# Trunk kernel in fp32r parts: one tile for a weight's high and low parts, eighteen block products in the wide form, parameters turned behind the last unit

## The chip, the cores and the metric

The kernel runs on 1 core of one Trainium2 chip. The metric is the device time of one execution in microseconds. The core's engines are TensorE (PE, matmuls; PEld, its weight loads), VectorE (DVE), ScalarE (ACT), GpSimd (POOL) and SyncE (SP); transfers run on DMA engines and are issued here by SyncE (loads) and GpSimd (accumulating transfers from on-chip memory to on-chip memory).

## The reference

The input x has 512 tokens of 1024 values, in float32. There are two layers. Each adds a mixer and then a gated feed-forward network (FFN, 2816 hidden values) to the residual stream; each of these starts with an RMS norm, and a final norm ends the trunk.

```python
proj = gelu(einsum('bsd,de->bse', xn, w_in_odd[i]))          # mixer of layer 1
u, v = proj[..., :C_WIDTH], proj[..., C_WIDTH:]              # 1024 each
mix = chunked_spatial_gating(u, v, sgu_norm[i], w_spatial[i], b_spatial[i])
h = h + einsum('bse,ed->bsd', mix, w_out_odd[i])

def gated_conv_ffn(x, w_gate, w_up, conv_w, conv_b, w_down):
    g = einsum('bsd,df->bsf', x, w_gate)
    g = causal_dwconv3(g, conv_w) + conv_b
    up = einsum('bsd,df->bsf', x, w_up)
    return einsum('bsf,fd->bsd', silu(g) * up, w_down)
```

## The kernel before

**Arithmetic.** Every float32 matrix product is made from fp32r matmuls. An operand is split into a high part (the value rounded to fp32r) and a low part (the rest), and three matmuls, high by high, high by low and low by high, are summed in PSUM (mm3, L153 to L157). Weights are loaded by SyncE as float32 (`raw_...`, four buffers). `parts` (L147) makes the high part on ScalarE and the low part on VectorE. `summed` (L136) makes the low part without VectorE: ScalarE writes the negated high part into it (L140), GpSimd issues a DMA that accumulates the float32 value onto it (L142), and ScalarE writes the high part (L144). High and low parts are tiles of their own, of tags `whi` and `wlo`, six buffers each.

**Block products.** The large products of the FFN's gate and up (key g and u) and of the mixer of layer 1 are made by a scheme of seven block products in place of eight (numbered 1 to 7; products 3, 5, 6 and 7 need sums of weight blocks, s12 and s34, and sums of activation blocks, t). One block product takes four steps of the contraction and has 256 token columns. `multiply` (L554) has two forms. The narrow one is mm3 four times, 12 matmuls of 256 columns (L577). The wide one takes high and low part of the moving operand as one operand of 512 columns: four matmuls with the high part of the stationary operand (L567) and four of 256 columns with its low part (L570). Its sum stands in both halves of a PSUM bank, and who reads it has to add the two. Products 1, 6, 7 and 4 go to a bank "a", 5 and 3 to "e", 2 to "b" (BANK, L552). Seven banks are shared by all matmuls, and one is kept for transposes and the like.

**FFN.** The loop goes over units f = 0, 2, ..., 20, two 128-row tiles of the hidden dimension each. f=0 is computed directly, f=2 by narrow products, f=4 with wide gate and narrow up products, and f=6 and later by wide ones alone (FIRST_WIDE, L550; in_both, L794). Within a unit the products run in the order g1 u1 g5 g2 g6 u5 u6 u2 g7 u7 g3 u3 g4 u4 (`products`, L781). Results are collected by a copy on ScalarE and additions on VectorE (L800, L812) into `rows` (gate) and `kept` (up); then follow a causal convolution (c: ScalarE L611, VectorE L613), silu (L621), the factor 1/rms (rstd_f; s times r is L827), and the product with up, whose parts are the operands `a_hi` and `a_lo` of the down product (`d` in layer 0, `dn` in layer 1). `prepare` (L730 to L771) makes the weights of a unit: a11 (product 1), s12g, s34g, s12u, s34u and the second halves; s12g and s34g of f=4 and later get their low parts by the accumulating DMA (L758 to L760). A matmul is written g_8e if it belongs to gate, f=8, bank e.

**Mixer of layer 1.** v and u are 1024 columns each. The second half of v (v1) and the first half of u (u0) are made by seven block products for each of two token halves i (InProducts, L969 to L1030), all narrow; here the activations are stationary and the weights move. `v_0e` is v1, i=0, bank e.

**Parameters.** Each layer's norm and convolution parameters are loaded as rows, turned by one TensorE transpose (L110) and copied by VectorE (L112). Layer 1's are asked for at L888, behind the units of layer 0's FFN and ahead of d_last, the down product of its last four tiles.

**Order.** A scheduler puts the instructions of an engine in order, by their dependencies and its own estimates, except where `behind` (L83) or `inorder` ties one instruction behind another. So an edit at one place can move instructions at others. The last part of the kernel (L1340 on) is written out by hand: `taken` adds a down product to y (L1183), `squared`, `halved` (L1300), `rooted` and `inverted` make the final norm of a token block.

## Time and profile before

| | |
|---|---|
| median of 3 runs | 975.89 us (975.62 to 975.98) |
| the profiled execution | 975.82 us, of which the span of instructions is 974.1 us |
| TensorE clock granted | 0.999 |
| transposes of parameters (L110) | 2, at 32.7 and 227.6 us |
| low parts by accumulating DMA, s12g | 18 transfers, 4.5 to 7.8 us to landing |
| mean DMA rate | 152 GB/s |

In the rows quoted below a line of a timeline has start, duration, engine, line, operation, output and inputs, and, in brackets, how long the engine was idle before it and what ended the idle time. A line of the chain has start, the time it adds to the chain, engine, tile and line; "issue" is time in which the engine waited for nothing that the profile shows. Layer 0's FFN lies from about 150 to 470 us, layer 1's mixer around 475 to 630 and its FFN from there to the end.

### The profile page before, as it was taken

Reading aid. Unit: us, or ns where it says so; the run is one execution under the profiler, and the core shown is the slowest. Engines: PE = TensorE matmul, PEld = TensorE weight load, DVE = VectorE, ACT = ScalarE, POOL = GpSimd, SP = SyncE. Lnnn points to the kernel's source line nnn. Section 1 sums busy time; section 2 is a strip of 40 time slices with the busy share of each in tenths; the row PEclk is TensorE's granted clock in tenths of the full one; section 3 lists DMA queues with packets and bytes.
Section 4 is the critical chain, followed back from the end, with each engine's and each line's share of the span. In section 5 each row is a group of like instructions: output and inputs, shape, how many; then the busy total and the mean of one; then the engine's idle time right before and its main releaser. Section 6 shows DMA issues by size and latency. Waiting matters only on the chain.

```text
span 974.1 us, 14029 instructions
## 1 busy us (share of the span) xinstructions
PE 964.4 (99%) x5144; PEld 829.1 (85%) x5144; DVE 816.9 (84%) x1387; ACT 596.8 (61%) x905; POOL 149.6 (15%) x173
## 2 busy tenths in 40 slices
PE   9999999999999999999999999999999999999996
PEld 7888888998888888888889988889988888888885
DVE  5887458989899998998887765589898989889897
ACT  5523347765676555765488734587665666656775
POOL 2141023110111011110310001221111011110123
PEclk9999999999999999999999999999999999999999
DMA  7442225776777677764324623167767777668775
GB/s 251 143 141 86 87 87 111 178 176 164 194 167 167 167 170 195 170 164 152 120 62 116 202 77 100 55 131 188 185 145 195 195 173 165 170 159 200 194 156 137
DMA packets 94417, 148.36 MB, mean 152 GB/s; under 512 B 5156, under 2 KB 60428, under 8 KB 94348
## 3 DMA queue, kind: packets, MB, share of 16 engines
q1 hardware_dynamic: 78316, 98.69, 32.1%
q0 software_dynamic: 14256, 46.93, 26.8%
q10 hardware_dynamic: 1776, 1.84, 0.5%
q8 instruction: 40, 0.66, 0.3%
q14 instruction: 29, 0.24, 0.1%
HBM read 98.42 MB, written 2.10 MB: 103 GB/s over the span
## 4 chain that ended last, share of the span: by engine, by line
PE 98%; DVE 1%; issue 0%; ACT 0%; POOLq 0%; DVEq 0%; POOL 0%
PE d L156 3%; PE dn L156 3%; PE dn L157 3%; PE d L157 3%; PE dn L155 3%; PE d L155 3%; PE gu L155 2%; PE gu L157 2%; PE oo L157 1%; PE gu L156 1%; PE oo L156 1%; PE oo L155 1%; PE oe L157 1%; PE oe L156 1%; PE oe L155 1%; PE u_2a L577 1%
## 5 line engine op out<-in xcount | busy, mean ns | idle before, releaser
L613 DVE SCALAR_TENSOR_TENSOR c<-rows,prm,c 128x512 f32<-128x512 f32 x88 | 65.8, 749 | 2.6 <-ACT c L611 1.5
L142 POOL DMA_DIRECT2D wlo_g<-raw_g x20 | 17.2, 859 | 313.2 <-DVE kept L800 146.4
L156 PE MATMUL dn<-wlo_dn,a_hi 128*128 128x512 f32 x144 | 56.2, 390 | 0.0
L156 PE MATMUL d<-a_lo,whi_d 128*128 128x512 f32 x144 | 56.2, 390 | 0.0
L157 PE MATMUL dn<-whi_dn,a_lo 128*128 128x512 f32 x144 | 56.2, 390 | 0.0
L157 PE MATMUL d<-a_hi,wlo_d 128*128 128x512 f32 x144 | 56.2, 390 | 0.0
L155 PE MATMUL dn<-whi_dn,a_hi 128*128 128x512 f32 x144 | 56.1, 390 | 0.0
L155 PE MATMUL d<-a_hi,whi_d 128*128 128x512 f32 x144 | 56.1, 390 | 0.0
L727 ACT ACTIVATE whi_a<-raw_g 128x512 fp32r<-128x512 f32 x20 | 12.6, 632 | 58.4 <-PE g_8e L567 8.5
L211 POOL TENSOR_TENSOR ssq_f<-ssq_f,sq_f 128x512 f32<-128x512 f32 x14 | 19.4, 1386 | 135.4 <-ACT sq_f L210 100.4
L140 ACT ACTIVATE wlo_g<-raw_g 128x1024 fp32r<-128x1024 f32 x20 | 21.2, 1061 | 29.1 <-PE g_2e L577 8.7
L200 ACT ACTIVATE hg<-h,prm 128x512 fp32r<-128x512 f32 x24 | 17.3, 722 | 34.8 <-DVE h L313 34.8
L621 ACT ACTIVATE s<-c,prm 128x512 f32<-128x512 f32 x44 | 31.5, 718 | 9.6 <-DVE c L613 9.5
L1183 DVE SCALAR_TENSOR_TENSOR y<-dn,small,y 128x512 f32<-128x512 f32 x40 | 28.0, 750 | 7.4 <-PE dn L157 7.4
L611 ACT ACTIVATE c<-rows,prm 128x512 f32<-128x512 f32 x44 | 31.4, 715 | 4.1 <-DVE rows L824 4.1
L201 DVE SCALAR_TENSOR_TENSOR hg<-h,prm,hg 128x512 fp32r<-128x512 f32 x24 | 23.6, 986 | 11.1 <-ACT hg L200 11.1
L157 PEld LDWEIGHTS d<-a_hi,wlo_d 128*128 128x128 f32 x144 | 27.0, 188 | 5.7
L157 PEld LDWEIGHTS dn<-whi_dn,a_lo 128*128 128x128 f32 x144 | 27.0, 188 | 5.7
L155 PEld LDWEIGHTS d<-a_hi,whi_d 128*128 128x128 f32 x144 | 27.1, 188 | 5.4
L155 PEld LDWEIGHTS dn<-whi_dn,a_hi 128*128 128x128 f32 x144 | 27.1, 188 | 5.4
L156 PEld LDWEIGHTS dn<-wlo_dn,a_hi 128*128 128x128 f32 x144 | 27.0, 188 | 5.4
L156 PEld LDWEIGHTS d<-a_lo,whi_d 128*128 128x128 f32 x144 | 27.0, 188 | 5.4
(1132 smaller groups left out, 3317.6 us busy)
## 6 DMA issues: line engine op xcount, KB each, us to landing
raw_g<-in_w_ffn_gate_dram SPq DMA_DIRECT2D x40, 512.0 KB, 4.0
raw_u<-in_w_ffn_up_dram SPq DMA_DIRECT2D x40, 512.0 KB, 3.8
raw_dn<-in_w_ffn_down_dram SPq DMA_DIRECT2D x22, 512.0 KB, 5.9
wlo_u<-raw_u POOLq DMA_DIRECT2D x21, 512.0 KB, 6.7
wlo_g<-raw_g POOLq DMA_DIRECT2D x20, 512.0 KB, 4.6
raw_d<-in_w_ffn_down_dram SPq DMA_DIRECT2D x18, 512.0 KB, 6.0
wlo_s12g<-s12g POOLq DMA_DIRECT2D x18, 512.0 KB, 6.1
wlo_s34g<-s34g POOLq DMA_DIRECT2D x18, 512.0 KB, 6.0
```

What stands on the lines that cost most here:

```text
L140: first = nc.scalar.activation(lo, raw, AF.Copy, scale=-1.0)
L142: nc.gpsimd.dma_start(lo, raw, accum_op=ALU.add)
L155: nc.tensor.matmul(ps, lhs[0], rhs[0], start=start, stop=False)
L156: nc.tensor.matmul(ps, lhs[0], rhs[1], start=False, stop=False)
L157: nc.tensor.matmul(ps, lhs[1], rhs[0], start=False, stop=stop)
L200: nc.scalar.activation(hg[k][0], h[k], AF.Copy, scale=g)
L201: nc.vector.scalar_tensor_tensor(hg[k][1], h[k], g, hg[k][0].bitcast(F32), op0=ALU.mult, op1=ALU.subtract)
L211: nc.gpsimd.tensor_tensor(self.ssq, self.ssq, sq, ALU.add)
L611: nc.scalar.activation(c, t[:, 0:S], AF.Copy, scale=prm("cf", ft))
L613: self.last_conv = nc.vector.scalar_tensor_tensor(c, t[:, i : S + i], prm("cf", i * NF + ft), c, op0=ALU.mult, op1=ALU.add)
L621: self.last_silu = nc.scalar.activation(s, c, AF.Silu, bias=self.prm("bf", ft))
L1183: return nc.vector.scalar_tensor_tensor(dst, ps, ffn.cols[:, t : t + 1], dst, op0=ALU.mult, op1=ALU.add)
```

## The change

High and low parts of a weight become one tile of tag `w` with six buffers, of the same size as the two before. A buffer is claimed and given back for both parts together. For the mixer's v1 and u0 the products 2, 5 and 3 take the wide form, with the weights' two parts as the moving operand, and the places that collect them add both halves. In the FFN the up products 2, 5 and 3 of f=4 become wide as well, in both layers; their second additions are those that `after` makes already for wide products. Layer 1's parameters are turned behind the last matmul of the last unit (f=20) of layer 0, by a tie on TensorE. At the end `taken(5, 1, right)` moves ahead of `halved` and `rooted` of block 2. TensorE has 5069 matmuls and transposes in the program where it had 5141, VectorE 1407 instructions where it had 1389; ScalarE's, GpSimd's and SyncE's counts are as before.

```diff
--- before.py
+++ after.py
@@ -74,11 +74,11 @@
             ("ffn", rows_of(norm_ffn[0]), NK), ("cf", conv_rows(conv_ffn[0]), 3 * NF),
             ("bf", rows_of(b_conv_ffn[0]), NF)])
 
-    def params1():
+    def params1(order):
         return params("1", [
             ("mix", rows_of(norm_mix[1]), NK), ("bsp", b_spatial[0], NK),
             ("ffn", rows_of(norm_ffn[1]), NK), ("cf", conv_rows(conv_ffn[1]), 3 * NF),
-            ("bf", rows_of(b_conv_ffn[1]), NF)])
+            ("bf", rows_of(b_conv_ffn[1]), NF)], order)
 
     def behind(ins, first):
 
@@ -93,8 +93,8 @@
     for t in range(PAD):
         nc.gpsimd.memset(inv_pos[:, t : t + 1], 1.0 / (t + 1))
 
-    def params(layer, rows_):
-        return params_fetch(layer, rows_, nc.sync)()
+    def params(layer, rows_, order=lambda ins: ins):
+        return params_fetch(layer, rows_, nc.sync)(order)
 
     def params_fetch(layer, rows_, queue):
         rows = sum(n for _, _, n in rows_)
@@ -109,7 +109,9 @@
             ps = aux_bank(f"prm_ps{layer}")
             order(nc.tensor.transpose(ps[:, :rows], pk[:rows, :], ident[:rows, :rows]))
             sb = cp.tile([P, P], F32, tag="prm0" if layer == "0" else "prm1", name=f"prm{layer}")
-            order(nc.vector.tensor_copy(sb[:, :rows], ps[:, :rows]))
+            ins = nc.vector.tensor_copy(sb[:, :rows], ps[:, :rows])
+            if order is inorder:
+                order(ins)
 
             def col(key, i):
                 return sb[:, views[key] + i : views[key] + i + 1]
@@ -133,10 +135,17 @@
     def weights(src, a, b, name):
         return parts(*fetch(src, a, b, name))
 
+    both_parts = {}
+
+    def part_tiles(name, *shape):
+
+        t = wp.tile([P, 2, *shape], F32R, tag="w", bufs=6, name=f"w_{name}")
+        both_parts[name] = t
+        return t[:, 0], t[:, 1]
+
     def summed(raw, a, b, name, between=lambda: None, after=None):
 
-        hi = wp.tile([P, a, b], F32R, tag="whi", bufs=6, name=f"whi_{name}")
-        lo = wp.tile([P, a, b], F32R, tag="wlo", bufs=6, name=f"wlo_{name}")
+        hi, lo = part_tiles(name, a, b)
         first = nc.scalar.activation(lo, raw, AF.Copy, scale=-1.0)
         behind(first, after)
         nc.gpsimd.dma_start(lo, raw, accum_op=ALU.add)
@@ -145,8 +154,7 @@
         return hi, lo
 
     def parts(raw, a, b, name, after=(None, None)):
-        hi = wp.tile([P, a, b], F32R, tag="whi", bufs=6, name=f"whi_{name}")
-        lo = wp.tile([P, a, b], F32R, tag="wlo", bufs=6, name=f"wlo_{name}")
+        hi, lo = part_tiles(name, a, b)
         behind(nc.scalar.activation(hi, raw, AF.Copy), after[1])
         behind(nc.vector.tensor_tensor(lo, raw, hi.bitcast(F32), ALU.subtract), after[0])
         return hi, lo
@@ -392,8 +400,7 @@
                     keep_busy(mm_bank("busy"), *STAY)
                 if k in raws:
                     raw, a, b, name = raws.pop(k)
-                    hi = wp.tile([P, a, b], F32R, tag="whi", bufs=6, name=f"whi_{name}")
-                    lo = wp.tile([P, a, b], F32R, tag="wlo", bufs=6, name=f"wlo_{name}")
+                    hi, lo = part_tiles(name, a, b)
                     for i in range(a):
                         zchunks[k + i] = hi[:, i, :], lo[:, i, :], raw[:, i, :]
                 whi, wlo, wraw = zchunks[k]
@@ -551,6 +558,8 @@
 
     BANK = {1: "a", 6: "a", 7: "a", 4: "a", 5: "e", 3: "e", 2: "b"}
 
+    last_matmul = [None]
+
     def multiply(banks, name, product, left, right, both=None):
 
 
@@ -567,8 +576,8 @@
                 nc.tensor.matmul(banks[at], left(kp)[0], both(kp), start=first and kp == 0,
                                  stop=kp == NP - 1, skip_group_check=True)
             for kp in range(NP):
-                nc.tensor.matmul(ps, left(kp)[1], right(kp)[0], start=False, stop=kp == NP - 1,
-                                 skip_group_check=True)
+                last_matmul[0] = nc.tensor.matmul(ps, left(kp)[1], right(kp)[0], start=False,
+                                                  stop=kp == NP - 1, skip_group_check=True)
             return banks[at]
         for kp in range(NP):
             (a_hi, a_lo), (b_hi, b_lo) = left(kp), right(kp)
@@ -720,8 +729,7 @@
                             (lambda kp: self.moving_both(product, kp)) if both else None)
 
         def unit(self, name):
-            return [wp.tile([P, 2, 4, P], F32R, tag=f"w{x}", bufs=6, name=f"w{x}_{name}")
-                    for x in ("hi", "lo")]
+            return part_tiles(name, 2, 4, P)
 
         def halves(self, hi, lo, src):
             nc.scalar.activation(hi, src, AF.Copy)
@@ -792,7 +800,7 @@
             s = {}
 
             def in_both(key, product):
-                return f >= FIRST_WIDE[key]
+                return f >= FIRST_WIDE[key] or f == FIRST_WIDE["g"] and product in (2, 5, 3)
 
             def add(d, bank, halves):
                 ins = None
@@ -885,7 +893,7 @@
                         halves=(half,), tail=0)
 
             ffn.split_acts(ffn.steps(half_down))
-            prm1 = params1()
+            prm1 = params1(lambda ins: behind(ins, last_matmul[0]))
             nxt = Norm("m1", lambda k: prm1("mix", k))
             project("d0_last", w_ffn_down[0], ffn.acts, list(range(NF - 4, NF)), nxt)
             return nxt
@@ -983,7 +991,8 @@
 
                 def put(self, product, how, at):
                     raw, a, b, name = self.raw[at]
-                    self.stat[product] = how(raw, a, b, f"{name}_{product}")
+                    hi_lo = how(raw, a, b, f"{name}_{product}")
+                    self.stat[product] = *hi_lo, both_parts[f"{name}_{product}"]
 
                 def rest(self):
                     b11, b21, b12, b22 = (self.raw[at][0] for at in
@@ -999,15 +1008,21 @@
                     self.put(3, parts, (1, 1))
 
                 def run(self, out_, done, behind_first):
+                    def add_both(dst, bank):
+                        for c in (0, HALF):
+                            nc.vector.tensor_tensor(dst, bank[:, c : c + HALF], dst, ALU.add)
+
                     banks = ({}, {})
                     e = {}
                     for i, product in ((0, 1), (1, 1), (0, 2), (1, 2), (0, 6), (1, 6), (0, 5),
                                        (0, 7), (1, 5), (1, 7), (0, 4), (0, 3), (1, 4), (1, 3)):
                         if (i, product) == (0, 2):
                             behind_first()
-                        hi, lo = self.stat[product]
+                        hi, lo, both = self.stat[product]
+                        wide = product in (2, 5, 3)
                         ps = multiply(banks[i], f"{self.name}_{i}", product, tokens(product, i),
-                                      lambda kp: (hi[:, kp, :], lo[:, kp, :]))
+                                      lambda kp: (hi[:, kp, :], lo[:, kp, :]),
+                                      (lambda kp: both[:, :, kp, :]) if wide else None)
                         c = {1: (0, 0), 2: (0, 0), 6: (0, 1), 3: (0, 1), 7: (1, 1), 5: (1, 1),
                              4: (1, 0)}[product]
                         dst = out_(i + 2 * c[0])[:, c[1] * HALF : (c[1] + 1) * HALF]
@@ -1017,13 +1032,13 @@
                             e[i] = ps
                         elif product == 7:
                             nc.scalar.copy(dst, ps)
-                            nc.vector.tensor_tensor(dst, e[i], dst, ALU.add)
+                            add_both(dst, e[i])
                             gelu(dst, dst, i + 2)
                         elif product == 4:
                             gelu(dst, ps, i + 2)
                             done(i + 2)
                         else:
-                            nc.vector.tensor_tensor(dst, ps, dst, ALU.add)
+                            add_both(dst, ps)
                         if product == 3:
                             row = out_(i)
                             gelu(row, row, i)
@@ -1355,9 +1370,9 @@
             taken(4, 0, left)
             squared(2, left)
             times(pool, 2, left)
+            taken(5, 1, right)
             halved(2, left, False)
             rooted(2)
-            taken(5, 1, right)
             squared(3, right)
             times(pool, 3, right)
             inverted(2)
```

The scheduler's order moves with it. GpSimd's and SyncE's orders stay as they were. On ScalarE the high part of the gate's second half (L144) now stands next to its low part (L140) in layer 0's units from f=8 on, ahead of the convolution's c (L611) where it came behind it. In layer 0, f=6's gate product 6 moves ahead of u_6e and u_6b, f=8's second instruction of s12g on VectorE moves behind s34g's first and s times r, and f=10's moves behind the split of the hidden tile 7. In layer 1's f=6 the gate product 6 is put between the matmuls of u_6e.

## The prediction

> **What bounds the kernel now.** I read the page first (busy shares and the chain that ended last), then TensorE's waits, then the chain and the engines' timelines around each edit. The columns of the first rows are busy time, share of the span and instructions; the last two give line, releaser, total wait, times and longest.
>
> ```profile
> PE 964.4 (99%) x5144; PEld 829.1 (85%) x5144; DVE 816.9 (84%) x1387; ACT 596.8 (61%) x905; POOL 149.6 (15%) x173
> PE 98%; DVE 1%; issue 0%; ACT 0%; POOLq 0%; DVEq 0%; POOL 0%
> PE z L439 <- ACT hg L407: 0.3, 1, 0.3
> PE dn_e L1277 <- DVE y L1183: 0.2, 1, 0.2
> ```
>
> The reader is to see two things. TensorE is busy 964.4 of 974.1 us and is 98% of the chain: what shortens the matmuls shortens the kernel, and there is hardly a wait to remove. And VectorE is at 84%, the only engine near it; an edit that hands it work can make TensorE wait where it does not wait now. The sum below is made against the profiled execution, 975.82 us with a span of 974.1; the median of the three runs is 975.89, so 0.07 us is added at the end. A measurement of this kernel can tell a change from none at about 0.2%, which is 1.95 us either way.
>
> **Eighteen products become wide.** Three products (2, 5 and 3) of each of two token halves of v1 and of u0 are 12; three of the up products of unit f=4 in each of two layers are 6. Each loses 4 of 12 matmuls. Layer 0's f=4 stands in the chain with both forms side by side: gate wide, up narrow.
>
> ```profile
> 200.79 1.44 PE u_4e L577 x12
> 205.11 0.93 PE g_4a L567 x4
> 206.04 0.47 PE g_4a L570 x4
> 206.51 1.43 PE u_4a L577 x12
> ...
> 544.62 1.44 PE u_0e L577 x12
> ```
>
> A narrow product takes 1.43 to 1.44 us, here and in the mixer; a wide one takes 0.93 + 0.47 = 1.40 (206.51 − 205.11). As many columns pass in both forms, so 72 matmuls fewer are worth only 0.03 to 0.04 us a product, −0.54 to −0.72 us for 18. I take −0.6: −0.4 in the mixer, −0.1 in each layer's f=4.
>
> The Trainium skill, "TensorE: Matmul & The Clock Gate", section "Back-to-back issue gap", gives a spacing of N/2.4 + 2.5 ns for an isolated matmul of N columns. By that a narrow product would be 12 x 109 = 1.31 us and a wide one 4 x 216 + 4 x 109 = 1.30, an estimate of −0.2 us for all 18 and a sum 0.4 us higher than mine; the rows show both forms longer and further apart, so they decide.
>
> **What VectorE pays.** A wide product leaves its sum in two halves of a bank, and one more 128x256 addition brings them together: 18 more.
>
> ```profile
> 228.03 0.42 DVE L800 TENSOR_TENSOR rows<-g_6e,rows 128x256 f32<-128x256 f32 x1
> 228.36 0.42 DVE L800 TENSOR_TENSOR rows<-g_6b,rows 128x256 f32<-128x256 f32 x1
> ...
> 204.30 0.69 DVE L728 TENSOR_TENSOR wlo_a<-raw_g,whi_a 128x512 fp32r<-128x512 f32 x1 [0.69 <-ACT whi_a L727]
> 206.55 0.89 DVE L800 TENSOR_TENSOR rows<-g_4a,rows 128x256 f32<-128x256 f32 x2 [0.43 <-PE g_4a L570]
> 217.07 0.69 DVE L313 TENSOR_TENSOR h<-d,h 128x512 f32<-128x512 f32 x1 [1.05 <-PE d L157]
> ```
>
> Additions start 0.33 us apart, so f=4 gains 1.0 us of VectorE work, and its idle of 0.69 + 0.43 + 1.05 = 2.2 us before 217.07 covers that; without the cover it would be 1.0 us in each layer. In the mixer six additions in v1 and six in u0 cost 2.0 us each.
>
> ```profile
> 546.09 0.42 DVE L1026 TENSOR_TENSOR u<-u_0e,u 128x256 f32<-128x256 f32 x1 [0.92 <-PE u_0e L577]
> 561.75 0.69 DVE L1073 TENSOR_TENSOR gt<-sp,g_bc 128x512 f32<-128x512 f32 x1 [3.87 <-PE sp L157]
> ```
>
> VectorE waits for TensorE there, 0.92 us in the middle of u0's last products and 3.87 us behind them. What can be late is a bank: the second addition of u0's product 3 ends about when TensorE wants that bank again. I price this at 0 to 0.5 us, take 0.2. Layer 1's f=6, behind its own f=4, is ordered anew by the scheduler in the same way; 0 to 0.3, take 0.15.
>
> **Parameters moved out of f=6.** Before, layer 1's parameters are transposed in the middle of layer 0's f=6.
>
> ```profile
> 226.07 0.93 PE u_6b L567 x4
> 227.00 0.72 PE u_6b L570 x4
> 227.72 0.10 PE prm_ps L110
> 227.82 0.11 issue
> 227.93 1.16 PE g_6a L567 x4
> ```
>
> The transpose and the gap behind it are 0.21 us. Beside it stand two stalls: 0.72 where four such matmuls take 0.47, and 1.16 where 0.93 is usual, 0.25 + 0.23 us. The transpose is paid again behind the last group (+0.2 there), with its copy on VectorE. That copy goes ahead of one low part of the last down weights, which d_last needs only with its fourth chunk. The scheduler also puts f=6 back into the order of the program (g_6a of product 6 ahead of u_6e, u_6b two products later), so both stalls should go. With f=4's 0.1 us TensorE comes to f=8 some 0.8 us earlier if nothing new stops it, between 0.3 and 0.8 if the reordered s12u and g_6a are tight (0 to 0.5).
>
> **High and low parts in one tile, and f=8.** Merging the tiles adds no instruction, but a slot now serves both parts, and the order shows what follows: ScalarE makes both parts of the gate's weights at once, where before the high part came after s12g. So everything behind them on ScalarE comes one activation later, first the convolution's c, for which VectorE's next instructions wait. And on VectorE, layer 0's f=8 has two more instructions (s34g's first, s times r) ahead of s12g's second. SyncE's and GpSimd's own orders do not change. These are the rows of before, VectorE, ScalarE, GpSimd, the landing times in that window and (x18) over the span, and the chain, with f=12's transfer and its use at the end:
>
> ```profile
> 238.44 0.75 DVE L613 SCALAR_TENSOR_TENSOR c<-rows,prm,c 128x512 f32<-128x512 f32 x1
> 244.49 0.70 DVE L750 TENSOR_TENSOR s12g<-s12g,raw_g 128x512 f32<-128x512 f32 x1
> 245.09 0.69 DVE L769 TENSOR_TENSOR s34g<-raw_g 128x512 f32<-128x512 f32 x1
> ...
> 236.62 1.06 ACT L140 ACTIVATE wlo_g<-raw_g 128x1024 fp32r<-128x1024 f32 x1 [2.36 <-PE u_6e L570]
> 237.63 0.72 ACT L611 ACTIVATE c<-rows,prm 128x512 f32<-128x512 f32 x1
> 245.25 1.04 ACT L758 ACTIVATE wlo_s12g<-s12g 128x1024 fp32r<-128x1024 f32 x1
> 246.20 1.05 ACT L760 ACTIVATE whi_s12g<-s12g 128x1024 fp32r<-128x1024 f32 x1
> ...
> 246.59 0.86 POOL L759 DMA_DIRECT2D wlo_s12g<-s12g  x1 [7.75 <-ACT wlo_s12g L758]
> ...
> wlo_s12g<-s12g POOLq DMA_DIRECT2D x1, 512.0 KB, 7.2
> wlo_s12g<-s12g POOLq DMA_DIRECT2D x18, 512.0 KB, 6.1
> wlo_s34g<-s34g POOLq DMA_DIRECT2D x1, 512.0 KB, 7.5
> ...
> 253.09 0.94 PE g_8e L567 x4
> 254.03 0.51 PE g_8e L570 x4
> ...
> 305.23 0.86 POOL L759 DMA_DIRECT2D wlo_s12g<-s12g  x1 [5.29 <-ACT wlo_s12g L758]
> ...
> 315.12 0.48 PE g_12e L570 x4
> ```
>
> Read it backwards. TensorE starts g_8e's low matmuls at 254.03, and the accumulating transfer that they need was issued at 246.59 and lands 7.2 us later, at 253.8: it is only just in time. It starts when ScalarE's low part of s12g is done, and that follows VectorE's s12g at once (245.09, 245.25). Now the new order. ScalarE's wlo_g waits for u_6e, which ends 0.1 to 0.8 earlier; behind it come the high part (0.95 from start to start, 245.25 to 246.20) and only then c. So c ends at 238.5 to 239.2 instead of 238.35, and VectorE's c starts up to 0.8 later than 238.44. From there to s12g's second instruction lay 6.05 us; with s34g and s (0.6 each, 244.49 to 245.09), less a few that have moved ahead of c, the queue I add up is 6.9. The second s12g then starts at 245.4 to 246.1, 0.9 to 1.6 late, and the transfer lands at 254.7 to 255.4 where TensorE would now be ready at about 253.25. I take 254.95 for the start of the low matmuls, +0.9 against 254.03, with f=4's gain and f=6's vanished stalls already used up in it. The bounds are −0.8 (the transfer is not late at all) and +1.7 (ready at 255.4, with a little more). f=10's s12g is moved later too, but to the place where f=12's is made now, which is issued 9.9 us ahead of its use (305.23, 315.12; the last two rows), against 7.4 in f=8: 0 to 1.0, take 0.1.
>
> The Trainium skill, "DMA: Bandwidth & Descriptors", section "Issuing engines are not separate DMA queues", says that transfers of different issuing engines share the same 16 engines and interleave. By that an accumulation that starts later meets the weight loads at another point, so its 7.2 us need not stay 7.2; the longest case is the second rival below.
>
> **The tail.** One product's addition is put ahead of an instruction for which VectorE waits.
>
> ```profile
> 962.27 0.21 DVE L1300 TENSOR_SCALAR ssf<-ssf 128x1 f32<-128x1 f32 x1 [0.79 <-ACT sqf L1294]
> 962.41 0.74 DVE L1183 SCALAR_TENSOR_TENSOR y<-dn_e,small,y 128x512 f32<-128x512 f32 x1
> ```
>
> The 0.79 us of idle time can take the 0.65 us of the addition. TensorE's 0.2 us wait for dn_e (first fence) goes, and VectorE's end moves with TensorE's last products: 0 to −0.3, take −0.15.
>
> **Sum.** To the end of f=8 +0.9; f=10 +0.1; parameters +0.2; layer 1 −0.1 + 0.15; mixer −0.4 + 0.2; tail −0.15. Together +0.9: 975.89 + 0.9 = 976.8 us.
>
> **The rivals.**
> First: the gains stay. If VectorE's c does not wait, or the transfer takes the usual time (median 6.1 of 18), f=8 is at −0.8 to 0 instead of +0.9. For it speaks that VectorE ran at 217 with 1.05 us to spare; against it, that 254.03 stood 0.2 us behind the landing already. Time: 975.89 − 0.8 + 0.2 + 0.05 − 0.3 − 0.15 = 974.9; with every stall at its good end 974.3.
>
> Second, on the other side: the late accumulation falls behind the next load of down weights. SyncE issues two around it,
>
> ```profile
> 245.85 2.73 SPq L130 DMA_DIRECT2D raw_d<-in_w_ffn_down_dram  x2
> ```
>
> the second by about 248.6, and s12g's bytes start to move near then in the new order. If they share the engines with it and with s34g's accumulation, s12g lands as late as s34g does now, near 256.9 (issued 2.85 us after it, 7.5 us on the way). The low matmuls then start 2.9 us later than 254.03, and the sum is 0.9 − 0.9 + 2.9: 978.8. It decides if the issue slips past about 248.2, 1.6 us. Against it: that is the end of my bounds.
>
> Third: the wide form gives nothing in the mixer, where the weights and not the activations are the moving side. The wide rows of before all have activations there, so no row excludes it. Then 0.4 of the 0.6 us is lost, 977.2; a narrow product takes 1.44 us in both places, so I expect no difference in the wide one either.
>
> **How the numbers follow.** Forecast 0.5, first rival 0.25, second 0.2, third 0.05. The likeliest case is 976.8, its own range 975.7 to 978.0. The first rival reaches to 974.3 and the second to 979.1; leaving out the outer tenth at each end gives 974.4 to 978.8. Faster by over 1.95 us (below 973.94) needs more than every gain I can find: 0.08. Slower (above 977.84): nearly all of the second rival and a tenth of the forecast's case, 0.25. No change: 0.67.
>
> **What would show it.** Wide products in the mixer at 1.40 us; f=6 of layer 0 without the 0.72 and 1.16; a wait of TensorE at g_8e's low matmuls for wlo_s12g of about 1.5 us; 0.2 us for the transpose near the last group; VectorE idle between f=4's products reduced by 1 us. If g_8e does not wait, the first rival holds. If TensorE waits for VectorE's additions in u0, or at a place that I have not named, the forecast is wrong in kind.

## The result, and the profile after

| | before | changed |
|---|---|---|
| median of 10 runs | 975.84 us (975.15 to 975.98) | 978.43 us (977.46 to 980.92) |
| ratio | | 1.0029, 95% interval 1.0019 to 1.0039 |
| profiled execution, span | 975.82 us, 974.1 us | 978.67 us, 976.9 us |

The change costs 2.6 us. The page of the changed kernel, its busy times and its chain, and TensorE's waits (line, releaser, total, times, longest):

```profile
PE 963.9 (99%) x5072; PEld 824.9 (84%) x5072; DVE 820.1 (84%) x1405; ACT 595.6 (61%) x905; POOL 150.5 (15%) x173
PE 87%; DVE 6%; DMA 2%; ACT 2%; issue 2%; POOLq 0%; POOL 0%; DVEq 0%; ACTq 0%
...
PE g_8e L579 <- DMA w_s12g<-s12g: 1.2, 1, 1.2
PE v_1e L576 <- DVE v L1013: 1.1, 1, 1.1
PE u_10b L579 <- DMA w_u<-raw_u: 0.7, 1, 0.7
PE u_0a L586 <- ACT u L1030: 0.6, 1, 0.6
```

TensorE's busy time falls by 0.5 us, as wide products should make it, and VectorE's rises by 3.2. But the chain is no longer TensorE's alone: 87% where it was 98%, and four waits that before does not have. (The share alone doesn't tell a loss: with one tile only, below, the chain has TensorE at 89% in an unchanged time. One wait sends the chain back along another engine for a long way.)

Where the time went is best read from where TensorE starts the same product in two traces. The table has, for each kernel, the start of the first matmul of the product in that kernel's profiled execution less its start before (first row, us). A step between two columns is what was won or lost between them. The first column is no gain or loss of the places compared here: by the first 33 us the traces already lie −0.38 to +0.31 us apart, ahead of every unit in the table, and that distance stays in all columns of a row. Whether it belongs to the kernel or to the execution is not shown. (dn_d is one of the last down products, near the end of the span.)

| kernel | g_2a | g_8a | g_10a | g_16a | v | u_0a | wst | g_8a, layer 1 | dn_d |
|---|---|---|---|---|---|---|---|---|---|
| before, start | 167.99 | 250.15 | 280.70 | 372.35 | 485.75 | 528.61 | 551.53 | 732.73 | 965.40 |
| changed | −0.38 | −1.15 | +0.26 | +1.50 | +1.67 | +2.76 | +3.44 | +3.14 | +2.69 |
| mixer narrow | +0.02 | −0.75 | +0.25 | +1.11 | +1.28 | +1.28 | +2.05 | +1.74 | +1.28 |
| f=4 narrow | +0.05 | −0.65 | −0.66 | −0.66 | −0.50 | +0.41 | +1.09 | +0.83 | +0.37 |
| one tile only | +0.06 | −0.64 | −0.28 | −0.28 | −0.12 | −0.12 | +0.62 | +0.40 | +0.40 |
| parameters and tail only | +0.30 | +0.30 | +0.29 | +0.29 | +0.46 | +0.46 | +0.50 | +0.30 | −0.15 |
| changed, s12g first | −0.34 | −0.86 | −0.84 | −0.79 | −0.62 | +0.04 | +0.72 | +0.38 | −0.07 |
| no second additions | +0.13 | −0.66 | −0.44 | −0.44 | −0.27 | −0.52 | +0.14 | −0.18 | −0.63 |
| tile, tail, sums on VectorE | −0.29 | −0.99 | −0.68 | −0.68 | −0.51 | −0.51 | −0.52 | −0.73 | −1.19 |

The changed kernel wins 0.8 us up to f=8, loses 1.4 in f=8, 1.2 in f=10 to f=14, 0.2 at d_last, 1.1 in v1, 0.7 in u0, and wins 0.3 and 0.45 in what follows. f=8 is the place that the prediction named. VectorE, ScalarE, GpSimd and the chain there, changed kernel:

```profile
238.34 0.74 DVE L622 SCALAR_TENSOR_TENSOR c<-rows,prm,c 128x512 f32<-128x512 f32 x1
245.27 0.68 DVE L758 TENSOR_TENSOR s12g<-s12g,raw_g 128x512 f32<-128x512 f32 x1
...
245.99 1.06 ACT L766 ACTIVATE w_s12g<-s12g 128x1024 fp32r<-128x1024 f32 x1 [1.68 <-DVE s12g L758]
...
247.35 0.86 POOL L767 DMA_DIRECT2D w_s12g<-s12g  x1 [9.57 <-PE d L165]
...
247.35 6.64 DMA w_s12g<-s12g
254.03 0.74 PE g_8e L579 x4
```

From c to s12g's second instruction lie 6.93 us where there were 6.05; ScalarE and the transfer follow at once, and g_8e's low matmuls start when the transfer lands. (That they start at 254.03 in both kernels is chance: this execution is 0.38 us ahead from its start, so they are 0.38 us late against before.) In f=10 it is another transfer that is late, w_u. GpSimd's issues and the landing times, before and then changed (the last row is TensorE's):

```profile
271.33 0.86 POOL L759 DMA_DIRECT2D wlo_s12g<-s12g  x1 [1.92 <-ACT wlo_s12g L758]
282.34 0.86 POOL L142 DMA_DIRECT2D wlo_u<-raw_u  x1 [1.04 <-PE g_10a L570]
...
wlo_u<-raw_u POOLq DMA_DIRECT2D x1, 512.0 KB, 6.7
```

```profile
277.91 0.86 POOL L767 DMA_DIRECT2D w_s12g<-s12g  x1 [8.25 <-ACT w_s12g L766]
280.99 0.86 POOL L767 DMA_DIRECT2D w_s34g<-s34g  x1 [2.22 <-ACT w_s34g L766]
283.41 0.86 POOL L151 DMA_DIRECT2D w_u<-raw_u  x1 [1.55 <-ACT w_u L149]
...
w_u<-raw_u POOLq DMA_DIRECT2D x1, 512.0 KB, 9.1
...
292.51 0.74 PE L579 MATMUL u_10b<-hg,w_u 128*128 128x256 f32 x4 [0.65 <-DMA w_u<-raw_u]
```

s12g's transfer goes out 6.6 us later and so runs beside the two others; w_u takes 9.1 us instead of 6.7. Two loads of down weights go out among them as well, from 279.06 on; before, they went out from 277.24 on. With f=4 narrow (an experiment below) s12g goes out at 270.79 and these loads from 272.98 on, and w_u takes 5.1 us. So w_u is slow in the crowd; which member of it slows it most was not separated.

In the mixer VectorE and ScalarE are late (VectorE, ScalarE, chain):

```profile
526.78 1.23 DVE L159 TENSOR_TENSOR w_u<-raw_u,w_u 128x1024 fp32r<-128x1024 f32 x1 [1.53 <-ACT w_u L158]
527.92 0.42 DVE L1013 TENSOR_TENSOR v<-v_1e,v 128x256 f32<-128x256 f32 x1
528.26 1.22 DVE L1002 TENSOR_TENSOR raw_u<-raw_u,raw_u 128x1024 f32<-128x1024 f32 x1
529.39 0.42 DVE L1013 TENSOR_TENSOR v<-v_1e,v 128x256 f32<-128x256 f32 x1
...
540.66 2.56 ACT L1069 ACTIVATE vnh<-v,rc_v 128x512 fp32r<-128x512 f32 x4 [0.97 <-DVE rc_v L262]
543.13 0.35 ACT L1030 COPY u<-u_0a 128x256 f32<-128x256 f32 x1
...
529.86 1.19 PE v_1e L576 x4
...
534.40 0.93 PE u_0b L576 x4
535.33 0.47 PE u_0b L579 x4
539.39 0.86 DVE ms_v L254
543.53 1.70 PE u_0a L586 x12
```

A wide product with moving weights takes 0.93 + 0.47 = 1.40 us like the others. But product 3 adds into the bank that still holds product 5, and so has to wait until both halves of it are read. These two additions have a 1.22 us instruction between them, the second ends at 529.81, and v_1e's next product starts at 529.86. u_0a starts when ScalarE's copy is done, and the copy stands behind four activations that waited for VectorE's rc_v. On the chain ahead of rc_v lies ms_v, an instruction on 128x4 values that takes 0.15 us before and 0.86 here; the last section shows beside what.

### The profile page after: what moved, and what is told of

Read it like the earlier page. It is cut to its first block, busy times and chain, and to the rows that moved or that the text cites. A ratio compares the mean times of both kernels' runs of the same rounds, so it can differ in the third digit from the quotient of the medians.

```text
span 976.9 us, 13859 instructions
## 1 busy us (share of the span) xinstructions
PE 963.9 (99%) x5072; PEld 824.9 (84%) x5072; DVE 820.1 (84%) x1405; ACT 595.6 (61%) x905; POOL 150.5 (15%) x173
## 4 chain that ended last, share of the span: by engine, by line
PE 87%; DVE 6%; DMA 2%; ACT 2%; issue 2%; POOLq 0%; POOL 0%; DVEq 0%; ACTq 0%
PE dn L164 3%; PE dn L165 3%; PE dn L163 3%; PE d L164 3%; PE d L165 3%; PE d L163 3%; PE gu L163 2%; PE gu L165 1%; PE oo L165 1%; PE gu L164 1%; PE oo L164 1%; PE oe L164 1%; PE oe L163 1%; PE oo L163 1%; PE oe L165 1%
## 5 line engine op out<-in xcount | busy, mean ns | idle before, releaser
L164 PE MATMUL dn<-w_dn,a_hi 128*128 128x512 f32 x144 | 56.2, 390 | 0.0
L165 PE MATMUL dn<-w_dn,a_lo 128*128 128x512 f32 x144 | 56.2, 390 | 0.0
L164 PE MATMUL d<-a_lo,w_d 128*128 128x512 f32 x144 | 56.2, 390 | 0.0
L165 PE MATMUL d<-a_hi,w_d 128*128 128x512 f32 x144 | 56.1, 390 | 0.0
L163 PE MATMUL d<-a_hi,w_d 128*128 128x512 f32 x144 | 56.1, 390 | 0.0
L163 PE MATMUL dn<-w_dn,a_hi 128*128 128x512 f32 x144 | 56.1, 389 | 0.0
L149 ACT ACTIVATE w_g<-raw_g 128x1024 fp32r<-128x1024 f32 x20 | 21.2, 1061 | 18.8 <-PE g_4e L579 8.4
L165 PEld LDWEIGHTS dn<-w_dn,a_lo 128*128 128x128 f32 x144 | 27.0, 188 | 5.7
L165 PEld LDWEIGHTS d<-a_hi,w_d 128*128 128x128 f32 x144 | 27.0, 188 | 5.7
L163 PEld LDWEIGHTS d<-a_hi,w_d 128*128 128x128 f32 x144 | 27.1, 188 | 5.4
L164 PEld LDWEIGHTS dn<-w_dn,a_hi 128*128 128x128 f32 x144 | 27.0, 188 | 5.4
L163 PEld LDWEIGHTS dn<-w_dn,a_hi 128*128 128x128 f32 x144 | 27.0, 188 | 5.4
L164 PEld LDWEIGHTS d<-a_lo,w_d 128*128 128x128 f32 x144 | 27.0, 188 | 5.4
L735 ACT ACTIVATE w_s34u<-s12u 128x1024 fp32r<-128x1024 f32 x20 | 21.2, 1062 | 16.5 <-DVE s12u L779 16.5
```

The source lines that it names most:

```text
L149: first = nc.scalar.activation(lo, raw, AF.Copy, scale=-1.0)
L163: nc.tensor.matmul(ps, lhs[0], rhs[0], start=start, stop=False)
L164: nc.tensor.matmul(ps, lhs[0], rhs[1], start=False, stop=False)
L165: nc.tensor.matmul(ps, lhs[1], rhs[0], start=False, stop=stop)
L735: nc.scalar.activation(hi, src, AF.Copy)
```

## The experiments

Every time below is a median of 11 runs, beside 975.55 to 975.74 us for the kernel before in the same sessions. Ratios are to that kernel.

**Mixer narrow.**

```diff
-                        for c in (0, HALF):
+                        for c in (0,):
...
-                        wide = product in (2, 5, 3)
+                        wide = False
```

> The changed kernel with the mixer's v1 and u0 products all narrow again; the rest of the change stays. Theory (the mixer's additions are paid by TensorE): the waits of TensorE before v_1e (1.2 us) and u_0a (0.8 us) go, the wide form's 0.4 us is given back, so about 1.7 us under the changed kernel: 976.7 us. The waits in f=8 and f=10 stay. Rival (the tile for both parts delays the mixer, not the additions): the waits of 1.2 and 0.8 us stay in at least half and the time is 978 to 979 us.

977.56 us, ratio 1.0019 (1.0010 to 1.0027). The time lies between the two ranges. The wait before v_1e is gone; the one before u_0a stays at 0.5 us. So theory and rival each had part of it: v_1e's wait needs the additions, u_0a's comes without them too. From v to wst the mixer still loses 0.77 us in the table.

**f=4 narrow.**

```diff
-                return f >= FIRST_WIDE[key] or f == FIRST_WIDE["g"] and product in (2, 5, 3)
+                return f >= FIRST_WIDE[key]
```

> The changed kernel with the up products 2, 5 and 3 of f=4 narrow again; the rest stays. Theory (the additions of f=4 move s12g of f=8 and f=10 behind other work, which makes their accumulating transfers late): no wait of TensorE for w_s12g in f=8 nor for w_u in f=10, together 2.0 us or more, less the 0.1 us of wide form: 976.2 to 976.7 us. Rival (the order of ScalarE under one tile makes them late): the waits stay at 1 us or more, 978.3 to 978.7 us.

976.42 us, ratio 1.0009 (1.0000 to 1.0018). Both transfers' waits are gone, and from g_8a to g_16a the table shows no loss. The theory holds: the wide form of three products in f=4 was enough to give s12g of f=8 and f=10 another place in the scheduler's order; without it s12g's second instruction stands ahead of s34g's first. (That it is their additions and not their matmuls, the kernel without second additions shows below.)

**One tile only.** The kernel before with `part_tiles` in place of the two tiles, nothing else.

> The kernel before with nothing but high and low parts in one tile. Theory: the new order of ScalarE alone costs TensorE less than 0.6 us, 975.3 to 976.5 us, with no wait over 0.5 us in f=8, f=10 and the mixer. Rival (the one tile makes the waits): 977.2 us or more, with at least one of the waits of f=8, f=10, v_1e and u_0a in place.

975.69 us, ratio 1.0003 (0.9994 to 1.0012), TensorE's waits:

```profile
PE u_0a L586 <- ACT u L1030: 0.5, 1, 0.5
...
PE g_8e L579 <- DMA w_s12g<-s12g: 0.2, 1, 0.2
```

The time is as the theory said, but the rival is right about one wait: u_0a's comes with the tile alone. And a gain of 0.7 us up to f=8 comes with it too, though nobody tied the parameters here: under one tile the scheduler itself puts the transpose at d_last.

**Parameters and tail only.** The kernel before, with separate tiles, with `params1` tied behind the last matmul and `taken(5, 1, right)` moved.

```diff
-            prm1 = params1()
+            prm1 = params1(lambda ins: behind(ins, last_matmul[0]))
...
+            taken(5, 1, right)
...
-            taken(5, 1, right)
```

> The kernel before with nothing but the parameters turned behind the last unit and the addition moved ahead at the end. Theory: f=6 of layer 0 loses the transpose's 0.2 us and the stall behind it, 0.2 us come back at the last unit, and the end gains the 0.4 us that it gained in the changed kernel: 0.4 to 0.9 us faster than before, 975.0 to 975.5 us. Rival (f=6 gained from the other order that came with the tile, and the end from noise): within 0.2 us of before, 975.6 to 976.1 us.

975.55 us, ratio 0.9999 (0.9991 to 1.0008): the rival. In f=6 TensorE waits for VectorE instead (chain, then its waits):

```profile
227.74 0.35 DVE rows L808
228.09 0.14 issue
228.23 1.16 PE g_6a L576 x4
...
PE g_6a L576 <- DVE rows L808: 0.5, 1, 0.5
```

The table has the same start of g_8a relative to g_2a as before, +0.2 us at d_last for the transpose, and −0.45 us at the end. Of these 0.45 us, 0.1 is lost again behind dn_d, and 0.3 us is what this execution was behind from its start, so the span is 974.1 us in both.

**s12g first.**

```diff
-                nc.vector.tensor_tensor(s12[:, 1], s12[:, 0], r0[:, :, :P], ALU.subtract)
+                twice = nc.vector.tensor_tensor(s12[:, 1], s12[:, 0], r0[:, :, :P], ALU.subtract)
...
-                behind(nc.vector.tensor_tensor(s34[:, 0], r0[:, :, :P], r0[:, :, P:],
-                                               ALU.subtract), self.added[key])
+                third = nc.vector.tensor_tensor(s34[:, 0], r0[:, :, :P], r0[:, :, P:],
+                                                ALU.subtract)
+                behind(third, self.added[key])
+                if by_dma:
+                    behind(third, twice)
```

> The changed kernel with one tie on VectorE: where s12g and s34g get their low parts by transfer, the first instruction of s34g goes behind the second of s12g. Theory (s12g's place on VectorE sets when the transfer lands): in f=8 of layer 0 s12g is done about 0.6 to 1.2 us earlier, TensorE's wait for w_s12g falls from 1.2 to between 0 and 0.6 us, and f=10's accumulating transfers, no longer crowded, make TensorE wait 0.3 us or less for w_u: 976.9 to 977.6 us. Rival (the loads of down weights set the landing): both waits stay within 0.3 us of what they are, 978.1 to 978.7 us.

976.90 us, ratio 1.0013 (1.0004 to 1.0022). Neither transfer makes TensorE wait. VectorE, GpSimd and the landing of w_u in f=10:

```profile
244.48 0.69 DVE L758 TENSOR_TENSOR s12g<-s12g,raw_g 128x512 f32<-128x512 f32 x1
...
246.57 0.86 POOL L767 DMA_DIRECT2D w_s12g<-s12g  x1 [8.42 <-ACT w_s12g L766]
275.28 0.86 POOL L767 DMA_DIRECT2D w_s12g<-s12g  x1 [6.66 <-ACT kept L848]
...
w_u<-raw_u POOLq DMA_DIRECT2D x1, 512.0 KB, 8.0
```

s12g is 0.8 us earlier on VectorE and its transfer is issued 0.8 us earlier, which is what f=8 lacked; in f=10 it goes out 2.6 us earlier and w_u needs 8.0 us, not 9.1. In the trace one tie of order removes 2.6 us of loss from g_8a to g_16a (−0.86 to −0.79 in place of −1.15 to +1.50). The median fell by only 1.5 us; the runs lie between 975.88 and 977.96, the profiled one being the fastest, and which part the others lose was not traced.

**No second additions.** The changed kernel with one addition per wide product, as for a narrow one, in f=4 and in the mixer. The products' second halves of columns are left out of the sums there.

```diff
-                halves = range(1 + in_both(key, product))
+                halves = range(1 + (f >= FIRST_WIDE[key]))
...
-                        for c in (0, HALF):
+                        for c in (0,):
```

> The changed kernel with its 18 new additions left out: the wide products are made, but the second half of the bank (activations' or weights' low part) isn't added for the new wide products of f=4 and of the mixer. Theory (the additions on VectorE, not the wide matmuls, make the new waits): no wait before v_1e, none for w_u in f=10, 0.1 to 0.4 us in f=8 and 0.5 to 0.8 us before u_0a as with one tile alone; 0.6 us from the wide form and 0.45 us from the end against one tile alone, so 974.4 to 974.9 us. Rival (a bank held by a wide product is free too late): the wait before v_1e stays at 0.7 us or more and the time is over 975.4 us.

974.92 us, ratio 0.9993 (0.9984 to 1.0001); the only wait left is u_0a's, 0.3 us. So the 72 matmuls fewer and the one tile together are harmless, and what costs is the 18 additions, 3.5 us with their consequences (978.43 − 974.92, medians of two sessions). In f=8 s12g's second instruction is ahead of s34g's first here too (243.95 and 244.55), with f=4's products wide: it is the additions that move it.

**Narrow with ties.** One tile, the tail, s12g's tie, and `v_normed(0)` called after product 6 of u0, where the kernels above call it ahead of u0; f=4 and the mixer are narrow.

```diff
...
+                        if (i, product) == (0, 5):
+                            behind_sixth()
...
-                v_normed(0)
...
-            u0.run(lambda t: u[0][:, t, :], lambda t: None, beside_u0)
+            u0.run(lambda t: u[0][:, t, :], lambda t: None, beside_u0,
+                   lambda: v_normed(0))
```

> No product is made wide beyond those of before; kept are the one tile and the earlier addition at the end; s12g's tie of the kernel above is put in, and the mixer's normed v (vnh, vnl, first half) is asked for behind product 6 of u0 in place of product 1, so that ScalarE copies u before it. Theory (u_0a waits only because ScalarE's copy stands behind four activations that wait for VectorE): the wait before u_0a falls under 0.2 us, and 0.45 us come from the end: 974.4 to 974.9 us, faster than before. Rival (the later vnl makes the spatial stage wait instead): 975.1 us or more, with a new wait before sp.

976.16 us, ratio 1.0006 (0.9997 to 1.0015): a miss. u_0a no longer waits, but TensorE waits 0.7 us before the second group of transposes of w_spatial, until VectorE has read the first out of the one bank that both use; VectorE gets to it at 555.39, with one tile only at 554.13. Putting ScalarE's copy first moved the wait and did not remove VectorE's lateness.

**Changed with ties.** The changed kernel with the two edits shown above, s12g's tie and the later `v_normed(0)`.

> The changed kernel with both orders of the two kernels with ties. Theory: the waits of f=8, f=10 and u_0a shrink as there, the one before v_1e stays at 0.9 to 1.2 us: 976.0 to 976.8 us. Rival (waits come back elsewhere): 977.4 us or more.

976.67 us, ratio 1.0009 (1.0000 to 1.0018): as the theory said, v_1e's wait of 1.0 us being the one left.

**Sums on VectorE.** What made VectorE late before u_0a? With one tile alone its hg instructions of the mixer's norm read thus, beside GpSimd's additions of squares, and, in the last fence, with those additions on VectorE:

```profile
472.84 3.42 DVE L209 SCALAR_TENSOR_TENSOR hg<-h,prm,hg 128x512 fp32r<-128x512 f32 x2
479.05 1.77 DVE L209 SCALAR_TENSOR_TENSOR hg<-h,prm,hg 128x512 fp32r<-128x512 f32 x1
...
472.71 1.29 POOL L219 TENSOR_TENSOR ssq_m<-ssq_m,sq_m 128x512 f32<-128x512 f32 x1 [39.62 <-ACT sq_m L218]
474.34 1.37 POOL L219 TENSOR_TENSOR ssq_m<-ssq_m,sq_m 128x512 f32<-128x512 f32 x1 [0.33 <-ACT sq_m L218]
478.28 1.99 POOL L219 TENSOR_TENSOR ssq_m<-ssq_m,sq_m 128x512 f32<-128x512 f32 x1 [2.57 <-ACT sq_m L218]
```

```profile
472.95 1.96 DVE L201 SCALAR_TENSOR_TENSOR hg<-h,prm,hg 128x512 fp32r<-128x512 f32 x2
```

```profile
472.44 0.74 DVE L209 SCALAR_TENSOR_TENSOR hg<-h,prm,hg 128x512 fp32r<-128x512 f32 x1
473.10 0.68 DVE L219 TENSOR_TENSOR ssq_m<-ssq_m,sq_m 128x512 f32<-128x512 f32 x1
473.70 0.74 DVE L209 SCALAR_TENSOR_TENSOR hg<-h,prm,hg 128x512 fp32r<-128x512 f32 x1
```

(The middle fence is before: the same two take 1.96 us.)

```diff
-                nc.gpsimd.tensor_tensor(self.ssq, self.ssq, sq, ALU.add)
+                (nc.vector if self.name == "m1" else nc.gpsimd).tensor_tensor(
+                    self.ssq, self.ssq, sq, ALU.add)
```

The first kernel with this edit is the kernel before with the one tile and with `taken(5, 1, right)` moved:

> One tile for both parts and the earlier addition at the end, nothing wide; and the seven additions of squares of the mixer's norm (ssq_m, GpSimd) are done on VectorE. Theory (with one tile two of VectorE's hg instructions fall beside GpSimd's additions and take 1.7 us in place of 0.75 and 1.2, VectorE goes 0.8 us late through the mixer and TensorE waits before u_0a): hg takes 0.75 to 0.8 us throughout, the wait before u_0a falls from 0.65 to under 0.2 us, 974.4 to 974.9 us. Rival (the long hg has another cause, or VectorE's seven more additions cost what they save): hg stays over 1.2 us in the mean, or the wait before u_0a stays over 0.4 us; 975.2 us or more.

974.72 us, ratio 0.9993 (0.9984 to 1.0002), the lowest median of all: 0.83 us under the kernel before in its session, though the interval includes 1. hg takes 0.74 to 0.75 us eight times out of eight, and no wait is left in the mixer. The theory holds for the cause; that the kernel is faster than before is not shown.

**Before with tail and sums.** The same without the one tile: separate tiles, `taken(5, 1, right)` moved, the sums' edit.

> The kernel before with the earlier addition at the end and the same seven additions on VectorE, separate tiles. Theory: the end gains 0.45 us and nothing else can, because no wait of the mixer is left there but 0.2 us before wst: 975.0 to 975.3 us. Rival (VectorE's additions delay the norm): 975.6 us or more, with a new wait between 464 and 510 us.

975.46 us, ratio 0.9998 (0.9990 to 1.0007): between the two, and not to be told from before. There is no new wait between 464 and 510 us; −0.2 us before the first sp and −0.45 at the end show in the trace and hardly in the median. Against this median the one of the kernel with the one tile is 0.7 us lower, as much as the one tile gained up to f=8.

**Changed, s12g first, sums.** The changed kernel with s12g's tie and the sums' edit.

> The changed kernel with s12g's tie and the seven additions on VectorE. Theory: the wait before u_0a falls from 0.8 to under 0.2 us and that before v_1e by half or more, as both follow VectorE's lateness: 975.4 to 976.1 us. Rival (v_1e waits for the second additions themselves): v_1e's wait stays at 0.7 us or more, 976.2 us or more.

975.66 us, ratio 1.0001 (0.9992 to 1.0010). v_1e's wait is gone altogether, so the second additions made TensorE wait only because VectorE came late to them. u_0a's wait stays at 0.5 us, which the theory did not have: beside VectorE's lateness it has a second cause.

**u0 narrow.** That kernel, with the mixer wide in v1 alone.

```diff
-                        for c in (0, HALF):
+                        for c in (0, HALF) if self.name == "v1" else (0,):
...
-                        wide = product in (2, 5, 3)
+                        wide = self.name == "v1" and product in (2, 5, 3)
```

> The kernel of the run before (changed, s12g's tie, squares summed on VectorE) with u0's products narrow again; v1 and f=4 stay wide. Theory (the wait that is left before u_0a, 0.6 us, is the price of u0's six additions): it falls under 0.2 us, 0.2 us of wide form is given back: 974.3 to 974.9 us, faster than before by 0.7 to 1.2 us. Rival (the wait comes from v1's additions or the ties): the wait stays at 0.4 us or more and the time is 975.4 us or more.

975.57 us, ratio 1.0003 (0.9994 to 1.0012). A miss: by the distance between two products u_0a's wait falls from 0.6 to 0.27 us, so u0's additions were more than half of it, but the median did not follow. Two rows say more of the rest. The chain to u_0a has ms_v again, with 0.86 us, where the run before has 0.17; GpSimd is busy beside it:

```profile
535.91 0.86 DVE ms_v L255
...
534.59 2.16 POOL L1128 TENSOR_SCALAR_AFFINE_SELECT ws<-ws 128x1024 f32<-128x1024 f32 x1 [14.96 <-issue]
```

And the gain in the trace is 0.76 us at dn_d but only 0.2 us in the span (973.9 us against 974.1): from dn_d to its end it takes 9.3 us, before takes 8.7 and most others 8.8. The run before has these 9.3 us too. Why is open, and no run takes ms_v's delay away alone.

## Why the prediction was right and wrong

The range (974.4 to 978.8) holds the time, but the forecast, 976.8 us and no change, was not what happened: the slowdown is 0.29%, clear of the noise (95% interval 0.19 to 0.39%), and slower had been given 0.25. That the range holds it is in part luck. The forecast's own case ended at 978.0; the range goes on to 978.8 for the second rival, whose collision did not happen. What carried the time there are f=10 to f=14 (1.2 us) and the mixer (1.8 us), which the sum had at +0.1 and −0.2. By the prediction's own last sign, a wait of TensorE at a place not named (v_1e; w_u in f=10), it is wrong in kind there. Term by term:

- **Wide products**, −0.6 us: right, in the mixer too (1.40 us); the third rival falls. TensorE's busy time, 0.5 us less, agrees.
- **Late transfer in f=8**, +0.9 to the end of f=8: right in mechanism, a little large in size. From g_2a to g_10a the changed kernel loses 0.64 us; 0.77 us had been gained up to g_8a, as forecast (0.8), and TensorE's wait is 1.2 us (about 1.5). The queue from c to s12g's second instruction was added up as 6.9 us and is 6.93. That instruction was forecast for 245.4 to 246.1 and starts at 245.27, or at 245.65 without the 0.38 us by which this execution is ahead. The size is off because the transfer took 6.6 us and not 7.2. The second rival's collision with the down weights needed an issue 1.6 us late; it was 0.8 us late, or 1.1 without the 0.38. The cause was taken from the order, and the order was given to one tile and f=4's additions together. It is the additions: with one tile alone the wait is 0.2 us, with f=4 narrow none. And the step that c, later on ScalarE, makes VectorE wait was wrong: VectorE comes to c 0.3 us late (238.34 against 238.44, and the 0.38), but with no idle time ahead of it, and ScalarE's c had ended at 238.18. The first rival's sum, 974.9, has a slip of its own: with the forecast's terms for the mixer (−0.2) and f=10 (+0.1) it would be 975.1.
- **f=10**, +0.1: wrong in size, 0.9 us there and 0.3 in f=12 to f=14. The step that failed is "issued 9.9 us ahead of its use", taken as 0 to 1.0 us. It looked at s12g's own transfer, which is in time; but the last of the three accumulating transfers that now run together, w_u, is slow (9.1 us), and it was not priced. The loss in f=12 to f=14 is seen in the changed kernel and again in the one with both ties, and not in the one with the mixer narrow; it is not explained.
- **Parameters**, stalls of f=6 gone and +0.2 us at d_last: the price is right (0.17) and so is the size of the gain, but it was credited to the wrong part. Moved alone, the transpose leaves TensorE waiting for `rows`; the gain of 0.7 us came with the one tile, whose order brings `rows` earlier.
- **Mixer**, −0.4 + 0.2: the step that failed worst, +1.8 us measured from v to wst. "VectorE waits for TensorE there" was read from idle times of 0.92 and 3.87 us near u0's end, and the wait in v1 was not priced at all: v_1e's bank has to be read twice before product 3 can add into it, and VectorE is already late in v1. With the additions left out, or with VectorE no longer late (squares summed on VectorE), this wait is gone. u_0a's wait was outside every term as well. It stands with one tile alone (0.5 us), because the tile's new order around d_last moves two hg instructions beside GpSimd's additions; u0's additions make one of their own, which is left when that is mended (0.5 us); and ms_v, on its chain, is 0.7 us longer in the changed kernel. How these add up there was not separated.
- **Layer 1 and tail**, +0.05 and −0.15: layer 1's f=4 and f=6 cost nothing (−0.10), and the tail gained 0.45 up to dn_d, as in every kernel that has the move; 0.1 of it is lost again behind dn_d. The prediction allowed up to 0.3.

## What to carry to other kernels

When an edit moves an order that a scheduler makes, cost the moved instructions by what stands behind them in another queue: here three additions in f=4 cost 2 us from two units later on (978.43 − 976.42), through transfers that were issued late, and one tie gave it back in the trace. Look also at the transfers that a moved one will run beside: in f=10 it landed in time itself, and another did not. And idle time of an engine near the end of a stage does not show that it has time at its beginning; look at when it arrives there.

## What the runs showed of the hardware

VectorE's hg (two inputs in on-chip memory) takes 0.75 us, and 1.77 when a GpSimd addition of 1.3 to 2.0 us runs at the time; moved to VectorE, seven such additions took 0.68 us each and made all hg of this norm short. The Trainium skill, "SBUF — State Buffer", section "SBUF: two separate sides", says that VectorE and GpSimd share one pair of ports under an exclusive lock, also where a VectorE instruction has two inputs in that memory and the GpSimd instruction reads it. The trace agrees: hg is longer by 1.02 us.

A tiny instruction is hit too. In the changed kernel the multiplication of 128x4 values (L254) falls beside GpSimd's masking of w_spatial (first row: before; then changed):

```profile
535.50 0.15 DVE L246 TENSOR_TENSOR ms_v<-ms_v,rc_v 128x4 f32<-128x4 f32 x1
...
539.39 0.85 DVE L254 TENSOR_TENSOR ms_v<-ms_v,rc_v 128x4 f32<-128x4 f32 x1
...
538.31 1.91 POOL L1124 TENSOR_SCALAR_AFFINE_SELECT ws<-ws 128x1024 f32<-128x1024 f32 x1 [15.88 <-DVE u L1013]
```

It ends 0.02 us after the masking. The fourteen traces separate the two cases: where the masking runs at the time (changed, f=4 narrow, s12g first, changed with ties, u0 narrow) it takes 0.85 us and ends within 0.02 us of the masking, in the other nine 0.15 to 0.16.

An accumulating transfer of 512 KB took 4.5 us when alone (f=10 of the changed kernel, w_g, issued at 268.81), and up to 9.1 us as the third of three issued within 5.5 us, with two loads among them.
